# Small parameters and sinks issued from GpSimd's queue, the sinks negated after the second norm, normed activations written for both token halves by one instruction

## The chip, the core and the metric

The kernel runs on one core of a Trainium2 chip. The metric is the device time of one execution in microseconds, as the median of several runs; lower is better. One further execution was recorded by the hardware profiler, and all rows below come from it.

## What is computed

One layer of a hybrid encoder, for 512 prompt tokens and 128 sample tokens (8 requests of 16), D = 1024, everything in float32:

```python
x = x + 0.5 * swiglu(rms_norm(x, norm_ffn1), w_ffn1_up, w_ffn1_down)      # FF = 2816
h = rms_norm(x, norm_mix);  P = h @ w_in                                  # 10752 columns
A = sliding-window attention(q, k, v, sinks)                              # 16 heads of 64
B = HGRN2 recurrence;  C = conv(4) -> RG-LRU * gelu gate
x = x + (sig(gA)*A@w_attn_o + sig(gB)*B@w_hgrn_o + sig(gC)*C@w_lru_o) @ w_out
x = x + 0.5 * swiglu(rms_norm(x, norm_ffn2), w_ffn2_up, w_ffn2_down)

def sink_softmax(s, sinks):
    m = max(max(s), sinks)
    p = exp(s - m)
    return p / (sum(p) + exp(sinks - m))
```

The sinks are one learned number per head; the kernel needs them, and their negatives, in the attention stage only.

## The kernel before

All activations lie transposed: features on the 128 partitions, the T = 640 tokens (512 and 128) on the free axis, in 8 tiles of features. A product is made as two halves of 320 tokens (`HT`), each in its own PSUM bank (`pp`, four banks). Precision comes from splitting: a float32 matrix is rounded to a high part (`wh`, a cast) and a rest (`wl`, a subtraction), and three matmuls (high by high, high by rest, rest by high) replace one. So each weight block of 128 columns (`proj`) is loaded (`wr`, three buffers), cast (L743, on ScalarE or VectorE), subtracted (L744, on VectorE), and multiplied by 24 matmuls (4 feature tiles) or 48 matmuls (8).

Each SwiGLU is made in four chunks of the hidden columns (`CHUNKS`: 4, 6, 6 and 6 blocks). The first chunk uses plain `proj`; the others use a scheme of seven products for eight (`pair`) that reads sums and differences of quarter blocks of the normed activations. These are prepared by `combos`, after the first block of the first chunk: it writes the normed activations x * gain * rstd into buffers `vx`, in two instructions per feature tile, one for each half of the tokens, and then makes sums, casts and rests of them.

Small parameters (norm gains, convolution, gates, q and k norms: 13 transfers) are loaded into a staging tile by `load_params`, called through `more_params` by `ffn` before block 4, and after block 8 is begun its `place` transposes them on TensorE (L441) into the tile `PRM`. They wait for RS, the first norm's result. The sinks go into the tile `SK` by 10 transfers in `attention`, each of which broadcasts numbers that lie 8 bytes apart to 16 or 64 partitions; they wait for `PRM`. One VectorE instruction (L374, called from `attention`) then writes the negated sinks.

The order of all instructions is not written by hand. Each call records an operation with its engine, its assumed duration and its data dependencies; `Sched.run` then plays a list schedule: at each step it takes the operation that could start first, by its assumed costs, and among those within 0.04 us the one with the best priority, and emits it. So the order on each engine is fixed when the program is built, by the planner's times and not by real ones, and each engine runs its list in order: if the first instruction of a list waits, all behind it wait. In this order the negation of the sinks stands on VectorE among the down-projections of the first chunk, long before the attention stage, because the planner takes the sinks to have landed by then. All transfers but one parameter load are issued by the SP queue (`dma`, L413), which is in order too.

Of the kernel before, what the change touches and what calls it, by code (L numbers as in the profile page):

```python
# [16 lines left out]
P = 128  # L17
# [139 lines left out]
class Sched:  # L157
# [4 lines left out]
    LAT_PE = 0.24  # L162
    LAT_TO_PE = 0.55
    LOAD = 1.35
    TO_R = 0.09
    RESIZE = 0.1

# [96 lines left out]
    def run(self):  # L264
        engines = ("PE", "DVE", "ACT", "POOL", "SP")
        free = dict.fromkeys(engines, 0.0)
        ready = {e: {} for e in engines}
        loaded, dma_free, mode = "none", 0.0, (True, P)
        tables = dict(TABLES, none=())

        def enlist(o):
            for a in o.alts:
                ready[a[0]][id(o)] = o

        for o in self.ops:
            if o.npred == 0:
                enlist(o)
        for _ in range(len(self.ops)):
            best = None
            for e in engines:  # L280
                cands = []
                for o in ready[e].values():
                    at, slots = (0.0, ()) if not o.news else self._place(o)
                    if at is not None:
                        sw = e == "ACT" and o.func is not None and o.func not in tables[loaded]
                        cands.append((max(free[e], o.ready, at) + (self.LOAD if sw else 0.0), o, slots))
                if not cands:
                    continue
                t0 = min(c[0] for c in cands)
                if best is not None and t0 >= best[0]:  # L290
                    continue
                near = [c for c in cands if c[0] <= t0 + 0.04]

                def key(c):
                    sw = e == "ACT" and c[1].func is not None and c[1].func not in tables[loaded]
                    if e == "PE" and c[1].mode[0] != mode:
                        return c[1].prio + 0.3 * 1e5
                    return c[1].prio + (0.35e5 if sw else 0.0)

                for c in sorted(near, key=key):  # L300
                    o = c[1]
                    if len(o.alts) > 1:
                        mine = c[0] + next(a[1] for a in o.alts if a[0] == e)
                        if min(max(free[a[0]], c[0]) + a[1] for a in o.alts if a[0] != e) < mine - 0.2:
                            continue
                    best = (c[0], e, o, c[2])
                    break
            if best is None:
                raise RuntimeError(self.stuck())
            start, e, o, slots = best  # L310
            dur, fn = next((a[1], a[2]) for a in o.alts if a[0] == e)
            if e == "ACT" and o.func is not None and o.func not in tables[loaded]:
                loaded = next(n for n, fs in TABLES.items() if o.func in fs)
            if e == "PE":
                start += self.TO_R if o.mode[0][0] and not mode[0] else 0.0
                start += self.RESIZE if o.mode[0][1] != mode[1] else 0.0
                mode = o.mode[1]
            end = start + dur
            free[e] = end
            if o.dma:  # L320
                dma_free = max(dma_free, start + 1.3) + o.dma / 250e3
                end = dma_free + 0.8
            for b, s in zip([b for b in o.news if b.slot is None], slots):
                b.slot, b.ap, s.owner = s, s.place(), b
                b.tag.next += 1
            for a in o.alts:
                ready[a[0]].pop(id(o), None)
            fn()
            o.done = True
            for b in o.bufs:  # L330
                b.left -= 1
                b.end = max(b.end, end)
                if b.left == 0 and b.slot is not None:
                    b.slot.owner, b.slot.free = None, b.end
            lat = self.LAT_PE if e == "PE" else self.LAT
            for s in o.succ:
                to_pe = s.alts[0][0] == "PE"
                s.ready = max(s.ready, end + (lat if not to_pe else 0.0 if e == "PE" else self.LAT_TO_PE))
                s.npred -= 1
                if s.npred == 0:  # L340
                    enlist(s)
# [3 lines left out]
def trunk_kernel(ctx: ExitStack, tc: tile.TileContext, A: dict, O: list):  # L345
# [12 lines left out]
    def act(n, f, aps=0, src=None):  # L358
        return ("ACT", 0.1 + 0.833e-3 * n + 0.093 * aps - (0.049 if src is not None and src.in_psum else 0.0), f)
# [25 lines left out]
    def fn(out, a, func, scale=1.0, bias=0.0, accum=None):  # L385
        aps = isinstance(scale, View) + isinstance(bias, View) + (accum is not None)
        kw = {}

        def f():
            if accum is not None:  # L390
                kw["accum_out"] = accum()
            nc.scalar.activation(out(), a(), func, bias=ap_of(bias), scale=ap_of(scale), **kw)  # L392

        return S.op([act(out.n, f, aps, a)], [a, scale, bias], [out] + ([accum] if accum is not None else []),
                    func=None if func in ANY_TABLE else func)

    def cp(out, a, only=None):
# [10 lines left out]
        alts = [pol(out.n, lambda: nc.gpsimd.memset(out(), val)), dve(out.n, lambda: nc.vector.memset(out(), val))]  # L408
        return S.op(pick(alts, only), (), [out])

    def dma(out, a, lag=None, after=(), act=False):
        v = out if isinstance(out, View) else a
        alts = [("SP", 0.47, lambda: nc.sync.dma_start(ap_of(out), ap_of(a)))]  # L413
        if act:
            alts = [("ACT", 0.47, lambda: nc.scalar.dma_start(ap_of(out), ap_of(a)))]
        return S.op(alts, [a, *after], [out], dma=v.n * 4 * v.proto.shape[0], lag=lag)

    def mm(calls):
# [82 lines left out]

    def combos_tags(sfx, ry, rx, at):

        S.tag("vx" + sfx, RW.slots(rx - 1, 0, T, 6) + of_ar(at, T, 4))
        S.tag("vB" + sfx, RX.slots(rx, 0, 2560, 2) + RY.slots(ry, 0, 2560, 1))
        arena(at, [("vS" + sfx, 512, 3), ("vr" + sfx, 1024, 1)])
        in_region(RW, rx, [("vh" + sfx, 512, 4), ("vl" + sfx, 512, 4)])
# [96 lines left out]
    def load_params(names, r0, r1, lag=None, act=False):  # L604
        b = S.buf("pst")
        later = () if act else (RS.v,)
        for name, r, c in (("norm_ffn1", 0, 8), ("norm_mix", 8, 8), ("norm_ffn2", 16, 8), ("conv_b", 24, 8),
                           ("conv_w", 32, 32), ("lru_b_a", 64, 8), ("lru_b_x", 72, 8), ("lru_lambda", 80, 8),
                           ("hgrn_lb_logits", 88, 8), ("hgrn_o_norm", 96, 1)):
            if name in names:  # L610
                src = A[name][0].rearrange("j (k p) -> (j k) p", p=P) if name == "conv_w" else A[name].rearrange("o (k p) -> (o k) p", p=P)
                dma(b[r - r0:r - r0 + c, 0:P].at(r), src, lag=lag, after=later, act=act)
        for r, name in ((97, "q_norm"), (98, "k_norm")):
            if name in names:
                for h in range(2):
                    dma(b[r - r0:r - r0 + 1, h * 64:h * 64 + 64].at((r, h)), A[name], lag=lag, after=later)

        def place():
            ps = S.buf("ml")
            n = r1 - r0  # L620
            tr([(ps[:, :n], b[:n, :P], ident[:n, :n])])
            cp(PRM[:, r0:r1].at(r0), ps[:, :n], only=("DVE",))

        if not act:
            return place
        place()
# [143 lines left out]
    def combos(norm, R, sfx):  # L770

        vs = [S.buf("vx" + sfx).v for _ in range(8)]
        for k in range(KD):
            h, q = k // 4, (k % 4) // 2
            for n in range(2):
                o = vs[(h * 2 + q) * 2 + n].r("p (a b) -> p a b", a=2)[:, k % 2, :].at(k % 2)
                stt(o, hv(xk(k))[:, n, :], prm(norm + k), hv(RS.v)[:, n, :], ALU.mult, ALU.mult)

        def x(h, n, q):
            return vs[(h * 2 + q) * 2 + n]

        def put(dst, q, v):
            hi, lo = dst(0, q), dst(1, q)
# [9 lines left out]
        vb = [in_b(S.buf("vB" + sfx)) for _ in range(3)]  # L795
        ops = {"x11": in_r(0), "x21": in_r(1), "x22": in_r(2), "t1": in_r(3), "t2": vb[0], "t3": vb[1], "t4": vb[2]}
        for q in range(2):
            a, b = S.buf("vx" + sfx), S.buf("vx" + sfx)
            tt(a.v, x(1, 1, q), x(0, 1, q), ALU.subtract)
            put(ops["t3"], q, a.v)  # L800
            tt(b.v, x(0, 1, q), x(0, 0, q), ALU.subtract)
# [165 lines left out]
    def attention():  # L967
        ck, cv = A["cache_attn_k"][0], A["cache_attn_v"][0]
        sk = A["attn_sinks"][0].rearrange("(m two) -> two m", two=2)
        for h in range(2):  # L970
            dma(SK[h * 64:h * 64 + 64, 0:8].at(h), sk[h:h + 1, :].to_broadcast([64, 8]), after=(PRM.v,))
            for b in range(4):
                p0 = b * 32 + h * 16
                dma(SK[p0:p0 + 16, 8:16].at((b, h)), sk[h:h + 1, :].to_broadcast([16, 8]), after=(PRM.v,))
        ts(SK[:, 16:32], SK[:, 0:16], -1.0, ALU.mult, only=("DVE",))
        ms = S.buf("ms")
        mi = S.buf("qt")
        i1, i2 = mi[:, 0:256].cast(I32), mi[:, 256:512].cast(I32)
# [504 lines left out]
```

## Time and profile before

| | us |
|---|---|
| median of 3 runs | 1932.46 (1931.64 to 1934.26) |
| the profiled execution, its own time | 1930.95 |
| its span, first to last instruction | 1929.1 |
| TensorE busy in it | 1895.8 (98%) |
| VectorE busy | 1388.1 (72%) |
| ScalarE busy | 740.3 (38%) |
| GpSimd busy | 36.4 (2%) |
| mean granted TensorE clock | 0.994 |

The 1.85 us between the span and the execution's own time lie around the first and last instruction. TensorE is the engine to look at: the span is its work plus the stretches in which it waits, and the stretches in which its clock is lowered. The other engines matter where they make it wait.

### The profile page before, as it was taken

To read this page: it belongs to the slowest core of one execution; us is meant where nothing else is said; L and a number is where in the kernel's file an instruction comes from. 1 tells how busy PE (TensorE), PEld (TensorE's weight loads), DVE (VectorE), ACT (ScalarE), POOL (GpSimd) and SP (SyncE) were. 2 spreads that over 40 slices of the span, in tenths; PEclk is the share of its full clock that TensorE was granted. 3 is DMA by queue.
4 is the path that set the end of the run, shared out by engine and by line. 5 is a ranking of instruction groups with operands and counts; after the bars stand their busy time and mean duration, and the time that the engine had idled before them with its cause. 6 is when DMAs were issued, how large, how long until landed. Compare 5 with 4: busy or idle time off the path is not lost.

```text
span 1929.1 us, 35224 instructions
## 1 busy us (share of the span) xinstructions
PE 1895.8 (98%) x14654; PEld 1851.0 (96%) x14654; DVE 1388.1 (72%) x2610; ACT 740.3 (38%) x1299; POOL 36.4 (2%) x63
## 2 busy tenths in 40 slices
PE   8899999999999999999999999999999999999999
PEld 8789999999999999999999999999999999999998
DVE  7788585877687773778547787886566989586784
ACT  6334141433477750776102343434112324142340
POOL 0000000000000000021000000000000000000000
PEclk9999999999999999999999999999999999999999
DMA  5133222225322112223221332232422133222322
GB/s 143 43 96 92 80 82 73 87 73 152 102 56 61 50 55 77 61 67 91 77 77 57 88 93 82 77 87 72 132 77 76 54 101 88 88 64 80 99 64 80
DMA packets 305130, 156.89 MB, mean 81 GB/s; under 512 B 22949, under 2 KB 302598, under 8 KB 304970
## 3 DMA queue, kind: packets, MB, share of 16 engines
q1 hardware_dynamic: 304954, 154.63, 27.8%
q8 instruction: 115, 1.88, 0.4%
q14 instruction: 45, 0.37, 0.1%
q10 hardware_dynamic: 16, 0.00, 0.0%
HBM read 143.32 MB, written 10.63 MB: 80 GB/s over the span
## 4 chain that ended last, share of the span: by engine, by line
PE 94%; DVE 2%; DMA 1%; ACT 1%; issue 0%; SPq 0%; DVEq 0%; ACTq 0%
PE pp L432 85%; PE me L432 4%; PE ml L432 3%; PE ml L441 1%; PE me L441 1%; DMA SK<-in_attn_sinks_dram 1%; DVE AR L368 1%; ACT AR L392 1%; DVE AR L1222 0%; ACT L392 0%; DVE AR L382 0%; DMA RX<-in_x_prompt_dram 0%; SPq L413 0%; DVE wl L744 0%; DVE RB L368 0%
## 5 line engine op out<-in xcount | busy, mean ns | idle before, releaser
L432 PE MATMUL pp<-RA,wh 128*128 128x320 f32 x4192 | 813.1, 313 | 0.3 <-DVE AR L368 0.3
L432 PEld LDWEIGHTS pp<-RA,wh 128*128 128x128 f32 x4192 | 658.1, 188 | 12.5 <-issue 9.5
L432 PE MATMUL pp<-RA,wl 128*128 128x320 f32 x2096 | 490.1, 309 | 4.5 <-DVE wl L744 4.5
L432 PE MATMUL pp<-RB,wh 128*128 128x320 f32 x2016 | 389.6, 310 | 13.5 <-DVE AR L382 12.7
L432 PEld LDWEIGHTS pp<-RA,wl 128*128 128x128 f32 x2096 | 354.0, 188 | 5.5 <-DVE wl L744 5.5
L432 PEld LDWEIGHTS pp<-RB,wh 128*128 128x128 f32 x2016 | 320.4, 188 | 14.8 <-DVE AR L382 13.3
L743 DVE CAST wh<-wr 128x1024 fp32r<-128x1024 f32 (+2 forms) x135 | 85.5, 633 | 237.5 <-PE pp L432 237.0
L432 PE MATMUL pp<-RB,wl 128*128 128x320 f32 x1008 | 241.9, 309 | 1.3 <-DVE wl L744 1.3
L744 DVE TENSOR_TENSOR wl<-wr,wh 128x1024 fp32r<-128x1024 f32 (+2 forms) x196 | 217.0, 1107 | 1.4 <-ACT wh L743 1.0
L831 ACT CAST RW<-AR 128x512 fp32r<-128x512 f32 x180 | 110.5, 621 | 259.6 <-PE pp L432 131.2
L432 PEld LDWEIGHTS pp<-RB,wl 128*128 128x128 f32 x1008 | 172.0, 188 | 1.5 <-DVE wl L744 1.5
L368 DVE TENSOR_TENSOR AR<-AR 128x640 f32<-128x640 f32 (+12 forms) x271 | 139.5, 519 | 24.8 <-ACT AR L392 15.7
L368 DVE TENSOR_TENSOR AR<-pp,AR 128x320 f32<-128x320 f32 x268 | 127.9, 486 | 34.4 <-PE pp L432 31.6
L392 ACT ACTIVATE AR<-AR 128x640 f32<-128x640 f32 (+2 forms) x184 | 110.6, 605 | 108.3 <-DVE AR L368 99.3
L432 PE MATMUL pp<-RX,RW 128*128 128x320 f32 x864 | 138.6, 309 | 0.0
L432 PEld LDWEIGHTS pp<-RX,RW 128*128 128x128 f32 x864 | 129.6, 188 | 0.0
L828 DVE TENSOR_TENSOR RW<-AR,RW 128x512 fp32r<-128x512 f32 x180 | 122.4, 686 | 2.0 <-ACT RW L831 0.7
L392 ACT ACT_TABLE_LOAD x72 | 92.4, 1283 | 2.5 <-PEq L1471 1.4
L743 ACT CAST wh<-wr 128x1024 fp32r<-128x1024 f32 (+2 forms) x61 | 59.7, 979 | 50.3 <-PE pp L432 49.9
L398 ACT COPY AR<-me 128x512 f32<-128x512 f32 (+3 forms) x74 | 26.8, 378 | 123.4 <-PE me L441 115.0
L382 DVE SCALAR_TENSOR_TENSOR AR<-pp,AR 128x320 f32<-128x320 f32 x128 | 61.4, 484 | 15.5 <-PE pp L432 15.5
L432 PE MATMUL pp<-RY,RW 128*128 128x320 f32 x432 | 69.2, 309 | 0.0
(184 smaller groups left out, 1953.1 us busy)
## 6 DMA issues: line engine op xcount, KB each, us to landing
wr<-in_w_in_dram SPq DMA_DIRECT2D x84, 512.0 KB
wr<-in_w_ffn_up_dram SPq DMA_DIRECT2D x52, 512.0 KB
AR<-in_w_ffn_up_dram SPq DMA_DIRECT2D x36, 512.0 KB
wr<-in_w_ffn_down_dram SPq DMA_DIRECT2D x48, 384.0 KB
wr<-in_w_ffn_down_dram SPq DMA_DIRECT2D x16, 256.0 KB
wr<-in_w_attn_o_dram SPq DMA_DIRECT2D x8, 512.0 KB
AR<-in_state_hgrn_dram SPq DMA_DIRECT2D x8, 512.0 KB
wr<-in_w_lru_o_dram SPq DMA_DIRECT2D x8, 512.0 KB
```

What stands on the lines that cost most here:

```text
L368: alts = [dve(out.n, lambda: nc.vector.tensor_tensor(out(), a(), b(), op=op))]
L382: return S.op([dve(out.n, lambda: nc.vector.scalar_tensor_tensor(out(), a(), ap_of(s), b(), op0=op0, op1=op1), isinstance(s, View))], [a, ...
L392: nc.scalar.activation(out(), a(), func, bias=ap_of(bias), scale=ap_of(scale), **kw)
L398: alts = [act(out.n, lambda: nc.scalar.copy(out(), a()), 0, a), dve(out.n * (1.0 if a.in_psum else 0.5), lambda: nc.vector.tensor_copy(out ...
L432: nc.tensor.matmul(o(), l(), m(), start=s, stop=e)
L441: nc.tensor.transpose(o(), i(), d())
L743: S.op([act(nk * P, lambda: nc.scalar.copy(h(), r())), dve(nk * P * 0.5, lambda: nc.vector.tensor_copy(h(), r()))], [r], [h], lag=2)
L744: S.op([dve(nk * P, lambda: nc.vector.tensor_tensor(l(), r(), h().bitcast(F32), op=ALU.subtract))], [r, h], [l], lag=1.5)
L828: S.op([dve(out.n, lambda: nc.vector.tensor_tensor(out(), a(), b(), op=op))], [a, b], [out], lag=lag)
L831: S.op([act(out.n, lambda: nc.scalar.copy(out(), a()))], [a], [out], lag=lag)
```

## The change

Four things change in the code.

1. The 13 parameter transfers and the 10 sink transfers are issued by GpSimd's queue (`small=True`, assumed cost 1.0 us each on POOL) instead of SP's. The first parameter load, norm_ffn1, stays on ScalarE's queue.
2. The negation of the sinks is recorded as reading RS as well as SK, after the second norm has written RS anew; so it can be planned only behind the second norm.
3. `combos` writes the normed activations with one instruction per feature tile for all 640 tokens (8 in place of 16, in each SwiGLU). The buffers `vx` become four of 2T in place of ten of T, and the two work buffers get a tag of their own, `vy`.
4. Two assumed costs of the planner change: no transfer lands before 5.5 us (`FIRST`), and a ScalarE instruction with an accumulated sum is taken as 0.1 us longer. No instruction is added by this; the emitted order can differ.

```diff
+    FIRST = 5.5
...
-        loaded, dma_free, mode = "none", 0.0, (True, P)
+        loaded, dma_free, mode = "none", self.FIRST, (True, P)
...
-        return S.op([act(out.n, f, aps, a)], [a, scale, bias], [out] + ([accum] if accum is not None else []),
+        alt = act(out.n, f, aps, a)
+        if accum is not None:
+            alt = (alt[0], alt[1] + 0.1, f)
+        return S.op([alt], [a, scale, bias], [out] + ([accum] if accum is not None else []),
                     func=None if func in ANY_TABLE else func)
...
-    def dma(out, a, lag=None, after=(), act=False):
+    def dma(out, a, lag=None, after=(), act=False, small=False):
...
+        if small:
+            alts = [("POOL", 1.0, lambda: nc.gpsimd.dma_start(ap_of(out), ap_of(a)))]
...
-        S.tag("vx" + sfx, RW.slots(rx - 1, 0, T, 6) + of_ar(at, T, 4))
+        S.tag("vx" + sfx, RW.slots(rx - 1, 0, 2 * T, 3) + of_ar(at, 2 * T, 1))
+        S.tag("vy" + sfx, of_ar(at + 2 * T, T, 2))
...
-                dma(b[r - r0:r - r0 + c, 0:P].at(r), src, lag=lag, after=later, act=act)
+                dma(b[r - r0:r - r0 + c, 0:P].at(r), src, lag=lag, after=later, act=act, small=not act)
...
-                    dma(b[r - r0:r - r0 + 1, h * 64:h * 64 + 64].at((r, h)), A[name], lag=lag, after=later)
+                    dma(b[r - r0:r - r0 + 1, h * 64:h * 64 + 64].at((r, h)), A[name], lag=lag, after=later, small=True)
...
-        vs = [S.buf("vx" + sfx).v for _ in range(8)]
+        vs = [S.buf("vx" + sfx) for _ in range(4)]
         for k in range(KD):
-            h, q = k // 4, (k % 4) // 2
-            for n in range(2):
-                o = vs[(h * 2 + q) * 2 + n].r("p (a b) -> p a b", a=2)[:, k % 2, :].at(k % 2)
-                stt(o, hv(xk(k))[:, n, :], prm(norm + k), hv(RS.v)[:, n, :], ALU.mult, ALU.mult)
+            o = vs[k // 2].v.r("p (n a b) -> p n a b", n=2, a=2)[:, :, k % 2, :]
+            stt(o, hv(xk(k)), prm(norm + k), hv(RS.v), ALU.mult, ALU.mult)
...
-            dma(SK[h * 64:h * 64 + 64, 0:8].at(h), sk[h:h + 1, :].to_broadcast([64, 8]), after=(PRM.v,))
+            dma(SK[h * 64:h * 64 + 64, 0:8].at(h), sk[h:h + 1, :].to_broadcast([64, 8]), after=(PRM.v,), small=True)
...
-        ts(SK[:, 16:32], SK[:, 0:16], -1.0, ALU.mult, only=("DVE",))
+        S.op([dve(16, lambda: nc.vector.tensor_scalar(SK[:, 16:32](), SK[:, 0:16](), -1.0, None, op0=ALU.mult))], [SK.v, RS.v], [SK.v])
```

## Rows read from the trace of the kernel before

**Rows 1.** The page: busy time of each engine; shares of the chain that ended last.
```profile
PE 1895.8 (98%) x14654; PEld 1851.0 (96%) x14654; DVE 1388.1 (72%) x2610; ACT 740.3 (38%) x1299; POOL 36.4 (2%) x63
...
PE 94%; DVE 2%; DMA 1%; ACT 1%; issue 0%; SPq 0%; DVEq 0%; ACTq 0%
```

**Rows 2.** Waits of PE, whole span: total us, times, longest.
```profile
PE pp L432 <- DVE AR L382: 12.7, 2, 12.3
PE pp L432 <- DVE wl L744: 5.7, 5, 2.7
PE me L441 <- DMA RX<-in_x_prompt_dram: 4.1, 2, 2.0
```

**Rows 3.** Windows by stage: length, busy us of each engine, clock, DMA share, GB/s.
```profile
core 0: us, PE busy (x) PEld busy (x) DVE busy (x) ACT busy (x) POOL busy (x), PEclk, DMA share, GB/s
...
31.00:75.00 44.00, 44.00 (x302) 43.99 (x301) 43.44 (x70) 18.76 (x27) 0.00 (x0) 1.00 0.22 62
...
88.15:107.60 19.45, 6.80 (x33) 6.45 (x33) 7.34 (x29) 0.21 (x1) 0.00 (x0) 0.65 0.25 68
107.60:117.60 10.00, 10.00 (x74) 9.81 (x72) 9.27 (x19) 4.02 (x6) 0.00 (x0) 1.00 0.59 173
125.00:475.00 350.00, 350.00 (x2388) 350.00 (x2388) 260.54 (x437) 124.99 (x198) 4.20 (x6) 1.00 0.31 90
...
790.00:903.00 113.00, 107.13 (x704) 105.28 (x703) 91.74 (x172) 92.05 (x119) 21.35 (x26) 0.97 0.22 64
```

**Rows 4.** Timeline of 74 to 101 us: start, us, engine, line, operation [idle before].
```profile
74.77 0.24 PE L441 MATMUL ml<-ident,AR 91*128 91x91 f32 x1
...
76.89 0.56 PE L432 MATMUL pp<-RB,wl 128*128 128x320 f32 x2 [1.25 <-DVE wl L744]
...
99.20 0.18 DVE L374 TENSOR_SCALAR SK<-SK 128x16 f32<-128x16 f32 x1 [15.42 <-DMA SK<-in_attn_sinks_dram]
...
100.44 0.64 PE L432 MATMUL pp<-RB,wh 128*128 128x320 f32 x1 [12.29 <-DVE AR L382]
```

**Rows 5.** The chain of waits, 70 to 105 us: start, us, what.
```profile
77.28 8.69 DMA SK<-in_attn_sinks_dram
...
89.86 9.11 DMA SK<-in_attn_sinks_dram
```

**Rows 6.** Windows of 2 us around the longest wait, columns as in the third group.
```profile
84.00:86.00 2.00, 2.00 (x16) 2.00 (x15) 0.00 (x0) 0.00 (x0) 0.00 (x0) 1.00 0.05 0
...
92.00:94.00 2.00, 0.00 (x0) 0.00 (x0) 0.00 (x0) 0.00 (x0) 0.00 (x0) 0.50 0.20 44
...
104.00:106.00 2.00, 2.00 (x13) 2.00 (x13) 1.56 (x9) 0.21 (x1) 0.00 (x0) 0.79 0.22 64
```

**Rows 7.** Timeline of the SP queue: parameter issues (first, last), then sink issues.
```profile
31.20 0.48 SPq L413 DMA_DIRECT2D AR<-in_norm_mix_dram  x1
...
35.92 0.55 SPq L413 DMA_DIRECT2D AR<-in_k_norm_dram  x2
...
77.28 4.85 SPq L413 DMA_DIRECT2D SK<-in_attn_sinks_dram  x7
82.23 0.39 SPq L413 DMA_DIRECT2D wr<-in_w_ffn_down_dram  x1
```

**Rows 8.** Timeline of DVE: normed activations by halves, and the nearest whole-width instruction.
```profile
1504.37 2.40 DVE L382 SCALAR_TENSOR_TENSOR RW<-AR,PRM,RS 128x320 f32<-128x320 f32 x5
...
16.64 1.68 DVE L382 SCALAR_TENSOR_TENSOR RA<-AR,PRM,RA 128x640 fp32r<-128x640 f32 x2 [0.83 <-ACT RA L392]
```

**Rows 9.** Timeline of PE in the second SwiGLU's first chunk.
```profile
1546.06 0.56 PE L432 MATMUL pp<-RA,wl 128*128 128x320 f32 x2 [1.22 <-DVE wl L744]
```

**Rows 10.** Instructions that read the tile SK: count, ns min/median/max, first and last start.
```profile
L376 DVE TENSOR_SCALAR AR<-AR,SK x40: 206/224/423, 525.9 to 695.4; 128x2 f32<-128x2 f32 x40
```

**Rows 11.** Line L392 on ACT: the extra instruction of an accumulated sum, startup.
```profile
L392 ACT ACTIVATION_READ_ACCUMULATOR AR<-RX x20: 185/187/216, 4.9 to 25.3; 128x1 f32 x20
```

**Rows 12.** Lines of DVE by form, 77 to 100 us: the casts of weight blocks.
```profile
L743 DVE CAST wh<-wr 128x512 fp32r<-128x512 f32 x3 | 1.3, 424 | 0.6 <-PE pp L432 0.5
```

More of the change, by code (lines that the diff above doesn't have):

```diff
@@ L770, in combos @@
     def combos(norm, R, sfx):
-        vs = [S.buf("vx" + sfx).v for _ in range(8)]
+        vs = [S.buf("vx" + sfx) for _ in range(4)]
         for k in range(KD):
-            h, q = k // 4, (k % 4) // 2
-            for n in range(2):
-                o = vs[(h * 2 + q) * 2 + n].r("p (a b) -> p a b", a=2)[:, k % 2, :].at(k % 2)
-                stt(o, hv(xk(k))[:, n, :], prm(norm + k), hv(RS.v)[:, n, :], ALU.mult, ALU.mult)
+            o = vs[k // 2].v.r("p (n a b) -> p n a b", n=2, a=2)[:, :, k % 2, :]
+            stt(o, hv(xk(k)), prm(norm + k), hv(RS.v), ALU.mult, ALU.mult)
         def x(h, n, q):
-            return vs[(h * 2 + q) * 2 + n]
+            return vs[h * 2 + q][:, n * T:(n + 1) * T]
         def put(dst, q, v):
@@ L797, in combos @@
         for q in range(2):
-            a, b = S.buf("vx" + sfx), S.buf("vx" + sfx)
+            a, b = S.buf("vy" + sfx), S.buf("vy" + sfx)
             tt(a.v, x(1, 1, q), x(0, 1, q), ALU.subtract)
@@ L970, in attention @@
         for h in range(2):
-            dma(SK[h * 64:h * 64 + 64, 0:8].at(h), sk[h:h + 1, :].to_broadcast([64, 8]), after=(PRM.v,))
+            dma(SK[h * 64:h * 64 + 64, 0:8].at(h), sk[h:h + 1, :].to_broadcast([64, 8]), after=(PRM.v,), small=True)
             for b in range(4):
                 p0 = b * 32 + h * 16
-                dma(SK[p0:p0 + 16, 8:16].at((b, h)), sk[h:h + 1, :].to_broadcast([16, 8]), after=(PRM.v,))
-        ts(SK[:, 16:32], SK[:, 0:16], -1.0, ALU.mult, only=("DVE",))
+                dma(SK[p0:p0 + 16, 8:16].at((b, h)), sk[h:h + 1, :].to_broadcast([16, 8]), after=(PRM.v,), small=True)
+        S.op([dve(16, lambda: nc.vector.tensor_scalar(SK[:, 16:32](), SK[:, 0:16](), -1.0, None, op0=ALU.mult))], [SK.v, RS.v], [SK.v])
         ms = S.buf("ms")
```

## The prediction

> **What bounds the kernel.** I read the page first. TensorE (PE) is busy 1895.8 of 1929.1 us and carries 94% of the chain that ended last [rows 1]. So the span is PE's work plus 33.3 us of idling, and a change can only pay where PE waits or runs at a low clock. The second view is the list of PE's waits: the largest entry is 12.7 us in two waits for VectorE (DVE) at L382, one of 12.3; next come 5.7 in five waits for weight rests [rows 2]. The third view is the windows by stage: from 31 to 75 us and from 125 to 475 us PE has no gap; 88.15 to 107.6 holds only 6.80 busy us in 19.45; 790 to 903 lacks 5.9 [rows 3].
>
> The long wait is then followed back. In the timeline PE starts again at 100.44 after 12.29 us idle; it waited for a DVE eviction, but DVE itself had stood 15.42 us before a tiny instruction at 99.20, the negation of the sinks, which waited for their transfers [rows 4]. The chain of waits shows these from 77.28 to 98.97 (89.86 + 9.11) [rows 5]. So ten transfers, 21.7 us from the first issue to the last landing, 2.17 each, block DVE's whole list, although their first reader starts at 525.9 [rows 10]. The reader should see that the engine named in PE's wait is not the culprit: the culprit is an instruction ahead of it in DVE's list whose data nobody needs yet.
>
> The clock adds to it. At 84 to 86 the granted clock is 1.00 (2.4 GHz), after some microseconds without matmuls 0.50 (1.2 GHz), and in 104 to 106 still 0.79 [rows 6]; PE, back at work from 100.44, is slow there.
>
> **The change part by part.**
>
> *Negation behind the second norm.* Its wait leaves the stretch. At full clock PE does 2388 matmuls in 350 us, 0.1466 each [rows 3]. In 88.15 to 107.6 it did 33, worth 33 x 0.1466 = 4.84 us, so 19.45 - 4.84 = 14.6 us are lost: the two idles of 12.7 and some 2 us of half clock [rows 2, 3, 6]. Is something else late in the gap? DVE was standing, not working, so its list simply moves forward. Right after, in 107.6 to 117.6, DVE does such work at 9.27 of 10 us with PE without a gap at clock 1.00 [rows 3], so DVE can feed PE, though with little room. The weight block that SP issued at 82.23 stood behind seven sink issues of 4.85 us [rows 7]; without them it goes out sooner, so weights are not late either. Term: -14.6, bounds -13.3 (with DVE's room so thin, one wait for a weight rest like the 1.25 us at 76.89 [rows 4] recurs) to -14.6. At its new place the instruction costs DVE at most its own 0.18 us [rows 4], somewhere near 480 to 526, where DVE is not known to hold PE: 0, bounds 0 to +0.2. Behind it stands the rest of DVE's attention work, but the sinks have been landed for hundreds of microseconds by then, unless GpSimd needs (525.9 - 77.3) / 10 = 45 us for each.
>
> *Sinks on GpSimd's queue.* SP loses 10 issues (two groups; the first seven 4.85 us [rows 7]). GpSimd's queue (POOL) gets 10 and has nothing else to do there: it is busy 36.4 us in all and idle in every stage from 31 to 118 us [rows 1, 3]. The same small packets still cross the same DMA engines, whose share in 84 to 86 was 0.05 [rows 6]. Cost 0, bounds 0 to +6 (the contention rival).
>
> *Parameters on GpSimd's queue.* SP loses 13 issues between 31.20 and 36.47 [rows 7]; PE had no gap until 75, so that gives 0. The receiver is the transpose at 74.77 in PE's list [rows 4]. From 31.20 that leaves 43.6 us, 3.35 for each of 13 if they go strictly one after another. No row shows a POOL-issued transfer. Nearest rows: 0.41 per issue on SP (5.27 / 13), below; 2.17 per sink transfer through landing, above [rows 5, 7]. At 2.17 the last lands at 31.2 + 28.2 = 59.4, 15 us early. Cost 0, bounds 0 to what the second rival says.
>
> The row that bears on interference: DVE is busy 43.44 of 44 us in 31 to 75, exactly where POOL would issue [rows 3]; the trace shows no POOL work there, so no interference can be read. The Trainium skill, page "SBUF — State Buffer", section "SBUF: two separate sides", speaks against this edit: descriptors of a transfer issued from GpSimd are written through a port that some VectorE copies hold, and it gives about 620 ns alone against about 3100 ns beside a float32 copy. By that figure the 13 would take 40.3 us and be done at 71.5 (an estimate from that page), 3.3 us before the transpose, and the sum would stand unchanged; no run here shows it yet.
>
> *Normed activations in one instruction.* Sixteen instructions of 320 columns become eight of 640, twice in the kernel. A run of five takes 2.40 us, 0.48 each; two of 640 columns with a per-partition scalar take 1.68, 0.84 each [rows 8]. So 16 x 0.48 - 8 x 0.84 = 1.0 us of DVE per SwiGLU. In the first one DVE is full up to the 1.25 us wait for a weight rest at 76.89 [rows 3, 4], so DVE's saving reaches PE: -1.0, bounds 0 to -1.25. In the second, the same wait is 1.22 us [rows 9], but more has happened between; I take -0.3, bounds 0 to -1.2.
>
> *Planner's costs.* The real extra instruction of an accumulated sum takes 0.187 us [rows 11], so the planner comes nearer to the truth; a late first landing shifts all its transfers alike and should leave their order. PE outside the long wait idles 33.3 - 12.7 = 20.6 us; a new order can shrink or stretch any of it. 0, bounds -3 to +3 (half the 5.9 of 790 to 903, each way).
>
> **Sum.** From the profiled execution's own 1930.95: -14.6 - 1.0 - 0.3 = 1915.05, 15.9 less. The median of the runs shown, 1932.46, lies 1.5 above that execution, so a median of 1932.46 - 15.9 = 1916.5. A measurement of this kernel tells about 0.2% (3.9 us) from no change.
>
> **Rivals.**
>
> *Contention: part of the gain is lost.* POOL's sink transfers hold up DVE's casts, or delay weight loads, just where PE used to stand. For it: DVE's room there is only 0.73 us in 10 [rows 3]. Against it: DMA share 0.05 [rows 6], and casts take only 0.42 us each [rows 12]. Price: in 21.7 us PE does 21.7 / (24 x 0.1466) = 6 weight blocks; if each cast waits for one transfer of 2.17 that is 13 us on DVE, less its room of 1.6, so up to 11.4; half of it, 5.7, gives 1922.
>
> *Parameters late: slower.* The transpose at 74.77 stands in PE's in-order list, all projections behind it. If a POOL transfer takes d, PE waits 13 d - 43.6 us; up to 3.35 it costs nothing, at 4.57 it eats the 15.9, and at 5 it costs 21.4, which gives 1938. For it: DVE is full then, and the last sink transfers took 9.11 us from issue to landing [rows 3, 5]. Against: that was latency and many small packets, while these are whole rows, and 13 in line at 2.17 are 15 us early. The Trainium skill's figure above lies just below the limit.
>
> *No change.* The negation goes, but another wait of that length appears: the DVE list held back by something else, or the order redrawn badly. Nothing in the rows names it; about 1931.
>
> *More gain.* The redrawn order also closes part of the 5.9 us in 790 to 903 [rows 3] and of the startup waits of 4.1 [rows 2]: 1910.
>
> **How the numbers follow.** Forecast (1912.5 to 1919.5, from -3 to +3 of the order) 0.65; contention (1919.5 to 1928) 0.15; more gain 0.08; no change 0.05; slower 0.07. The range 1911 to 1926 takes the forecast, most of contention and the near part of more gain: a little over 0.8. Faster by over 0.2% (below 1928.6): 0.65 + 0.15 + 0.08 = 0.88. Within: 0.05 and a little of the slower case, 0.06. Slower: 0.06.
>
> **What the new profile would show.** Right: the negation of the sinks stands after 478 us with no idle before it; PE's wait for L382 near 88 us is gone and the clock stays 1.00 from 31 to 118 us; 16 instructions of 640 columns write `vx` where 32 of 320 did; the parameter transpose has no wait before it. Wrong: PE waiting at a transpose L441 near 75 us (parameters late); DVE casts longer than 0.42 us or idle before them between 77 and 110 (contention); waits for weights there; or a longer list of PE's waits in 475 to 903 (order). If POOL's transfers take over 4.57 us each, the sign is wrong.

## The result

The changed kernel takes 1922.38 us, the median of 6 runs (1919.91 to 1924.02), against 1932.14 for the kernel before beside it (6 runs, 1930.95 to 1934.26). The ratio is 0.9946, with a 95% interval of 0.9936 to 0.9956: 9.8 us less, of the 15.9 forecast. The forecast was 1916.5, in a range of 1911 to 1926. The profiled execution took 1923.28 us, span 1921.5, which is 7.67 below the profiled execution of before (7.64 by the spans).

Page of the changed kernel, the row that answers to [rows 1] and the DMA queue that only kernels with transfers on POOL have (packets, MB, share of 16 engines):

```profile
PE 1898.9 (99%) x14654; PEld 1853.0 (96%) x14654; DVE 1389.1 (72%) x2599; ACT 735.8 (38%) x1295; POOL 44.3 (2%) x86
...
q0 software_dynamic: 736, 0.06, 0.4%
```

Its waits of PE over the whole span, which answer to [rows 2]:

```profile
PE pp L438 <- DVE wl L751: 6.4, 5, 2.4
PE me L447 <- DMA RX<-in_x_prompt_dram: 4.6, 2, 2.6
```

The long wait for an eviction is gone. The five waits for weight rests have grown from 5.7 to 6.4 us. PE's busy time has also grown, by 3.1 us with the same 14654 matmuls: part of the gain went into slower matmuls.

Windows by stage, with the columns of [rows 3]:

```profile
31.00:75.00 44.00, 44.00 (x304) 44.00 (x304) 41.14 (x60) 19.52 (x28) 0.53 (x1) 1.00 0.25 72
75.00:79.00 4.00, 2.41 (x18) 2.14 (x16) 4.00 (x7) 1.37 (x2) 0.00 (x0) 1.00 0.00 0
80.00:82.00 2.00, 2.00 (x10) 2.00 (x10) 2.00 (x6) 0.79 (x2) 0.00 (x0) 0.59 0.49 139
82.00:84.00 2.00, 2.00 (x10) 2.00 (x10) 1.60 (x6) 0.91 (x2) 0.00 (x0) 0.55 0.15 44
...
94.00:108.00 14.00, 14.00 (x100) 13.77 (x100) 12.47 (x26) 4.58 (x7) 0.00 (x0) 1.00 0.63 185
...
1538.00:1540.00 2.00, 2.00 (x10) 2.00 (x9) 2.00 (x6) 0.00 (x0) 0.00 (x0) 0.50 0.38 111
```

From 94 to 108 PE works without a gap at the full clock, where [rows 3] show 6.80 busy us in 19.45. New is what follows the waits for weight rests: from 80 to 84 the granted clock is 0.59 and 0.55 of 2.4 GHz, ten matmuls in 2 us where there would be sixteen, and 0.50 from 1538 on in the second SwiGLU.

Timeline of PE, then of DVE, around the first of these waits, and the negation's new place:

```profile
76.52 0.24 PE L447 MATMUL ml<-ident,AR 91*128 91x91 f32 x1
...
78.97 0.56 PE L438 MATMUL pp<-RB,wl 128*128 128x320 f32 x2 [1.59 <-DVE wl L751]
```

```profile
69.74 2.29 DVE L369 TENSOR_TENSOR RA<-RW,RA 128x640 fp32r<-128x640 f32 x3 [1.37 <-PE pp L438]
...
72.69 0.82 DVE L369 TENSOR_TENSOR RW<-RW 128x640 f32<-128x640 f32 x1
...
77.50 0.82 DVE L369 TENSOR_TENSOR RW<-RW 128x640 f32<-128x640 f32 x1
78.23 0.68 DVE L751 TENSOR_TENSOR wl<-wr,wh 128x512 fp32r<-128x512 f32 x1
...
468.31 0.17 DVE L980 TENSOR_SCALAR SK<-SK 128x16 f32<-128x16 f32 x1
```

The parameter transpose L447 waits for nothing; the negation stands at 468.31 with no idle before it. But DVE runs without a pause from 69.74, when PE releases rows of RA, to the weight rest at 78.23, and two subtractions within `RW` stand in that run, 0.82 us each. They come back below.

Timeline of the POOL queue (start, us):

```profile
2.85 0.66 POOL L421 DMA_DIRECT2D AR<-in_norm_mix_dram  x1 [1.54 <-PE ml L447]
...
11.32 0.96 POOL L421 DMA_DIRECT2D AR<-in_k_norm_dram  x2
12.27 1.81 POOL L421 DMA_DIRECT2D SK<-in_attn_sinks_dram  x3
...
32.15 0.53 POOL L421 DMA_DIRECT2D SK<-in_attn_sinks_dram  x1 [6.24 <-issue]
```

This is the surprise of the profile: the parameters are issued from 2.85 us on and the sinks from 12.27 to 32.15, not near 31 and 77 as on SP. `after=(RS.v,)` and `after=(PRM.v,)` order the planner's list, but the rows show no wait behind them: the first issue waits only for a transpose of the start, and the sinks go out long before PRM is written near 81. On SP the issues came late because they stood behind others in the queue. POOL's queue holds nothing else there, so they run at once.

**Where the time went.** The n-th of the 14654 matmuls can be set beside the n-th of before. The table gives by how much each stretch is longer (+) or shorter (-) than in the trace of before, in us, in one profiled execution of each kernel; the ranks 100, 500, 550, 650, 3400, 4750, 12000 and 12250 start at 23, 83, 106, 120, 524, 691, 1535 and 1573 us there. "sum - start" leaves out the first stretch, which varies for a reason that stays open (below). All thirteen are single executions; the medians stand beside them.

| kernel | to 100 | to 500 | to 550 | to 650 | to 3400 | to 4750 | to 12000 | to 12250 | sum - start | median us |
|---|---|---|---|---|---|---|---|---|---|---|
| changed | +1.75 | +1.88 | -14.92 | +0.01 | +0.01 | +1.48 | -0.04 | +2.18 | -9.40 | 1922.38 |
| e0 | +2.49 | +1.87 | -14.92 | +0.01 | 0.00 | +1.12 | -0.02 | +2.18 | -9.77 | 1923.52 |
| e1 | +1.45 | 0.00 | -14.92 | +9.36 | 0.00 | +0.01 | +0.82 | 0.00 | -4.72 | 1926.62 |
| e2 | +0.99 | +0.34 | -14.93 | +9.84 | -0.01 | +1.13 | -0.11 | +0.65 | -3.10 | 1930.28 |
| e3 | +1.05 | 0.00 | -14.93 | +0.01 | 0.00 | +1.20 | +0.92 | 0.00 | -12.82 | 1918.75 |
| e4 | +2.66 | +1.89 | -14.93 | +0.01 | +0.01 | +0.04 | +1.34 | +2.17 | -9.48 | 1920.51 |
| e5 | +1.27 | +0.34 | -14.92 | +6.40 | +0.01 | +1.14 | +0.19 | +2.18 | -4.67 | 1927.69 |
| e6 | +1.42 | -0.30 | -14.92 | +0.01 | 0.00 | +1.49 | +1.53 | 0.00 | -12.22 | 1918.49 |
| e7 | +2.43 | +0.01 | -14.92 | +0.01 | +0.01 | 0.00 | -0.08 | 0.00 | -15.00 | 1917.06 |
| e8 | -0.37 | -0.30 | -14.92 | +0.01 | -0.02 | -0.07 | -0.45 | 0.00 | -15.75 | 1916.18 |
| e9 | +1.91 | 0.00 | -14.92 | +0.01 | +11.73 | -0.02 | +1.73 | 0.00 | -1.50 | 1929.74 |
| e10 | +1.83 | 0.00 | -14.92 | 0.00 | -0.01 | -0.05 | -0.25 | +0.01 | -15.25 | 1916.94 |
| e11 | +0.72 | -0.30 | -14.92 | 0.00 | 0.00 | -0.04 | -0.44 | 0.00 | -15.72 | 1917.40 |

In the changed kernel's row the long wait is worth 14.92 us, and three things eat into it: 1.88 at the first wait for a weight rest, 1.48 in attention, 2.18 at the wait in the second SwiGLU. The experiments look for the cause of each.

### The profile page after: what moved, and what is told of

The parts are those of the page before. It is cut to its first block, busy times and chain, and to the rows that moved or that the text cites. A ratio compares the mean times of both kernels' runs of the same rounds, so it can differ in the third digit from the quotient of the medians.

```text
span 1921.5 us, 35215 instructions
## 1 busy us (share of the span) xinstructions
PE 1898.9 (99%) x14654; PEld 1853.0 (96%) x14654; DVE 1389.1 (72%) x2599; ACT 735.8 (38%) x1295; POOL 44.3 (2%) x86
## 3 DMA queue, kind: packets, MB, share of 16 engines
q8 instruction: 115, 1.88, 0.4%
## 4 chain that ended last, share of the span: by engine, by line
PE 93%; DVE 4%; ACT 2%; issue 1%; DMA 1%; SPq 0%; ACTq 0%; DVEq 0%
PE pp L438 84%; PE me L438 4%; PE ml L438 3%; PE ml L447 1%; PE me L447 1%; DVE AR L383 1%; ACT AR L393 1%; DVE AR L369 1%; DVE RB L369 0%; DVE AR L1227 0%; ACT L393 0%; DMA RX<-in_x_prompt_dram 0%; DVE wl L751 0%; SPq L417 0%; DVE RA L369 0%
## 5 line engine op out<-in xcount | busy, mean ns | idle before, releaser
L750 DVE CAST wh<-wr 128x1024 fp32r<-128x1024 f32 (+2 forms) x142 | 89.4, 630 | 237.2 <-PE pp L438 236.5
L750 ACT CAST wh<-wr 128x1024 fp32r<-128x1024 f32 (+1 forms) x54 | 53.7, 994 | 36.9 <-PE pp L438 36.5
```

The source lines that it names most:

```text
L750: S.op([act(nk * P, lambda: nc.scalar.copy(h(), r())), dve(nk * P * 0.5, lambda: nc.vector.tensor_copy(h(), r()))], [r], [h], lag=2)
```

## The experiments

**The negation alone.** e1 is the kernel before with only the negation's line changed:

```diff
-        ts(SK[:, 16:32], SK[:, 0:16], -1.0, ALU.mult, only=("DVE",))
+        S.op([dve(16, lambda: nc.vector.tensor_scalar(...))], [SK.v, RS.v], [SK.v])
```

> The kernel before with the negation of the sinks alone moved behind the second norm; everything else, all transfers on SP's queue too, as before. Theory A (the negation's move carries the whole gain, the other parts cost a little): the 12.3 us wait near 88 us and the half clock behind it go, 14.9 us less, so about 1917, 5 us below the changed kernel. Rival B (GpSimd's queue is needed as well: the ten sink issues still stand in SP's queue among the weight loads from 77 to 91 us): TensorE then waits some microseconds for a weight block between 85 and 105 us, and the time lies at 1920 to 1926.

Measured: 1926.62, ratio 0.9964 [0.9951, 0.9976]. The old wait is gone, and a new one of 6.93 us stands at 100.05: rival B's wait, at a time 0.6 us above its range. DVE of e1, its SP queue, the chain of waits (start, us, what) and a window of the DMA engines:

```profile
99.17 0.43 DVE L743 CAST wh<-wr 128x512 fp32r<-128x512 f32 x1 [10.01 <-DMA wr<-in_w_ffn_down_dram]
```

```profile
78.72 4.92 SPq L413 DMA_DIRECT2D SK<-in_attn_sinks_dram  x7
83.75 0.38 SPq L413 DMA_DIRECT2D wr<-in_w_ffn_down_dram  x1
87.42 5.06 SPq L413 DMA_DIRECT2D SK<-in_attn_sinks_dram  x3
```

```profile
83.75 15.33 DMA wr<-in_w_ffn_down_dram
```

```profile
84.00:92.00 8.00, 8.00 (x57) 8.00 (x56) 4.49 (x21) 0.00 (x0) 0.00 (x0) 1.00 0.05 0
```

The negation no longer waits for the sinks, but a cast now waits 10.01 us for a weight block. That block was issued at 83.75, behind the first seven sinks, and landed only 15.33 us later; from 84 to 92 the DMA engines were busy 0.05 of the time and moved 0 GB/s. The packet records show none of its packets on the move before 93. So it was not issued late: it stood behind the sinks' packets, on engines that were nearly idle. In the trace of before the same block went out at 82.23 [rows 7] while DVE stood until 99.20, so this second delay was hidden under the first. The transfers must move too.

**All on SP.** e2 is the changed kernel with the small transfers on SP (`if small:` replaced by `if False:`).

> The changed kernel with the 23 small transfers back on SP's queue. In the changed kernel's trace they were issued at 2.9 to 32 us, while the activations were loaded, and TensorE's list ran 1.75 us late from 45 us on. Theory A (small transfers among the first loads cost the startup): TensorE's 250th matmul starts at 45.0 as before instead of 46.7, 1.75 us less, about 1920.5. Rival B (the planner's new costs made the startup later): it stays at 46.7 and the time at 1922 or, if SP's queue is blocked by the sinks, above.

Measured: 1930.28, ratio 0.9985 [0.9977, 0.9994]: the loss of e1 is back (+9.84 in the table), as rival B allowed. On the start the run decides nothing (+0.99).

**The normed activations by halves.** e3 is the changed kernel with that part undone:

```diff
-        vs = [S.buf("vx" + sfx) for _ in range(4)]
+        vs = [S.buf("vx" + sfx).v for _ in range(8)]
...
+            for n in range(2):
+                stt(o, hv(xk(k))[:, n, :], prm(norm + k), hv(RS.v)[:, n, :], ALU.mult, ALU.mult)
```

> The changed kernel with the normed activations written by halves again, 16 instructions with the buffers of before. Theory A (the 1.0 us saved on VectorE is lost where it waits for TensorE to release the normed activations' old rows, before the wait for a weight rest): the waits for weight rests at 77 and 1535 us stay at 1.2 to 1.7 us, time within 2 us of the changed kernel, 1920 to 1924. Rival B (the forecast: VectorE's saving reaches TensorE): 1.3 to 2 us slower than the changed kernel, waits longer by 1 us each.

Measured: 1918.75, ratio 0.9922 [0.9909, 0.9936]. Both waits for weight rests are back at 1.26 and 1.22 us, the clock is 1.00 behind both, and the +1.88 and +2.18 of the table are 0. Neither theory had that: in these traces the one instruction for both halves did not save 1.3 us, it cost 4.1.

Most of the 4.1 is the clock, and not the waits themselves. e2 has the same instruction and the same first wait. PE of e2, and its window behind the wait:

```profile
78.21 0.56 PE L438 MATMUL pp<-RB,wl 128*128 128x320 f32 x2 [1.60 <-DVE wl L751]
```

```profile
80.00:82.00 2.00, 2.00 (x16) 2.00 (x15) 2.00 (x6) 1.54 (x3) 0.00 (x0) 1.00 0.26 63
```

Here the clock stays 1.00, also behind the second wait of 1.72, and the table has +0.34 and +0.65. So the longer waits cost 1.0 us together, and the fallen clock of the changed kernel 1.5 at each place.

**Why: a dependency that is none.** With both halves in one buffer, the subtraction that overwrites the second half is planned to wait for every reader of the buffer, the first half's too, which wait for PE to release RA. e6 is the changed kernel with one word more, by which a reader names its half:

```diff
-            return vs[h * 2 + q][:, n * T:(n + 1) * T]
+            return vs[h * 2 + q][:, n * T:(n + 1) * T].at(n)
```

> The changed kernel with the normed activations still made for both halves of the tokens in one instruction, but with their readers naming the half that they read, so that the subtraction of the two halves no longer has to wait until the first half's last reader is done. Theory A (this false dependency put the subtractions into the burst of VectorE ahead of wl and made wl late): the waits of PE for wl fall from 1.59 and 1.7 to 1.2 or less, the clock near 80 us and 1538 us stays at full speed, 1917.5 to 1919.5, the level of the kernel that makes them by halves (1918.75) or up to 1.3 less. Theory B (the whole-width instruction itself, or a cast that the planner gave to VectorE, makes wl late): the waits stay at 1.5 to 1.7 and the time at 1921 to 1923.

Measured: 1918.49, ratio 0.993 [0.9916, 0.9943], beside the changed kernel itself (e0: 1923.52, ratio 0.9952 [0.9939, 0.9964]): Theory A. Timeline of e6, DVE and then PE, and its window behind the wait:

```profile
64.64 0.82 DVE L369 TENSOR_TENSOR RW<-RW 128x640 f32<-128x640 f32 x1
...
69.42 2.30 DVE L369 TENSOR_TENSOR RA<-RW,RA 128x640 fp32r<-128x640 f32 x3 [1.33 <-PE pp L438]
...
77.42 0.68 DVE L751 TENSOR_TENSOR wl<-wr,wh 128x512 fp32r<-128x512 f32 x1
```

```profile
78.16 0.56 PE L438 MATMUL pp<-RB,wl 128*128 128x320 f32 x2 [1.10 <-DVE wl L751]
```

```profile
80.00:82.00 2.00, 2.00 (x16) 2.00 (x15) 1.78 (x5) 1.35 (x2) 0.00 (x0) 1.00 0.20 55
```

The subtractions stand ahead of the release of RA, the last at 64.64, where the trace of before has one at 64.26. The wait is 1.10 and the clock stays 1.00. The order alone did it: the instruction for both halves is still there. A cast of 0.42 us, which the changed kernel has on DVE at 74.16 within that run, went to ScalarE with the same edit, so its part and that of the two subtractions are not told apart.

> The changed kernel itself on the chip of the three kernels below, so that they can be compared with it: 1922.4 us before, expected 1921 to 1924. Its lateness at the 100th matmul against the first trace of the kernel before was +1.75 us; if that belongs to the transfers on POOL it comes again here and in the keyed kernel (+1.5 to +2), if it is the scatter of one execution it may be anything from 0 to 2.7.

e0's first 100 matmuls were 2.49 us late and e6's 1.42: scatter of that size leaves the question of the start open.

**The planner's costs.** e4 is the changed kernel with `FIRST` at 0 and without the 0.1 us for an accumulated sum.

> The changed kernel with the planner's two assumed costs as before (no first landing at 5.5 us, no 0.1 us more for accumulated sums). In the changed kernel the attention stage lost 1.5 us against the order of before (lead of 11.3 us at 490 us, 9.8 at 691). Theory A (the accumulated sums' new cost redrew that stage): the lead stays 11.3 us through the stage, about 1921. Rival B (the startup order was improved by the costs, or nothing depends on them): 1922 to 1924, lead 9.8 again.

Measured: 1920.51, ratio 0.9932 [0.9919, 0.9944]. The time is not told apart from the changed kernel's, but its loss in attention is, as Theory A had it: +0.04 instead of +1.48. In the table all six kernels with the 0.1 us (e0, e2, e3, e5, e6 and the changed one) lose 1.12 to 1.49 there, and all seven without it lose nothing. Hardly any wait is behind this (from 505 to 682 us e3 lists 0.2 us of PE waits) and the clock there is 1.00: the matmuls stand in another order. Which step of that order costs the time was not looked for. e7 takes e3's halves and the old cost of the sum together, and keeps `FIRST`:

> The changed kernel with the normed activations made by halves, as in the kernel before, and with the planner's old cost of an activation that sums; the negation behind the second norm, the transfers on POOL and the planner's first free time of the DMA stay. Theory A (the planner's cost cost 1.2 to 1.5 us in attention, and adds to the halves' gain): no loss between the 3400th and the 4750th matmul, 1916.5 to 1918, the fastest so far. Theory B (each plan is drawn anew and the two don't add): 1918 to 1921.

Measured: 1917.06 (1916.43 to 1918.38), ratio 0.9922 [0.991, 0.9935], attention 0.00: Theory A. e8 does the same with e6's one instruction:

> The changed kernel with whole-width normed activations whose readers name their half (1918.49 in the last call) and the planner's old cost of an activation that sums. Theory A (the two gains stand in different stages and add, as with the kernel by halves, which went from 1918.75 to 1917.06): 1916 to 1917.5, level with the kernel by halves or up to 1 us under it. Theory B (the one instruction for both halves saves nothing even without its false dependency, and the planner's cost changes where the plan was lucky): 1917.5 to 1920.

Measured: 1916.18 (1914.83 to 1917.22), ratio 0.9913 [0.99, 0.9927], the lowest median of all, though not told apart from e7's. Since e3 and e7 differ by the 0.1 us alone, and e6 and e8 too, this assumed cost is shown to be the cause.

**Queue or time.** e5 leaves the transfers on POOL but gives each group a real wait, a POOL copy of one column in front of it:

```diff
+        S.op([pol(1, lambda: nc.gpsimd.tensor_copy(GT.ap, RS[:, TP:TP + 1]()))], [RS.v], [GT.v])
...
+        S.op([pol(1, lambda: nc.gpsimd.tensor_copy(GS.ap, PRM[:, 8:9]()))], [PRM.v], [GS.v])
```

> The changed kernel with the small transfers still on POOL, but the parameters behind a POOL copy that reads the first norm's result, and the sinks behind a POOL copy that reads PRM, so that they are issued near 30 us and near 80 us, as on SP, and not from 2.9 us on. Theory A (what hurt in the kernel with the negation alone was SP's queue, in which the sinks stand ahead of the feed-forward weights): the weights are still issued early, no wait of PE for more than 2 us near 100 us, 1921 to 1924 as in the changed kernel. Theory B (the sinks' packets of 4 bytes slow the weights' packets on the DMA engines, whatever queue issues them): a wait of 4 to 7 us near 100 us is back, 1926 to 1929. Beside this: if the early transfers made the start 1 to 1.75 us late, the 100th matmul comes that much earlier here than in the changed kernel.

Measured: 1927.69, ratio 0.9977 [0.9968, 0.9986]: Theory B by the time. Here the sinks run where the forecast had put them, from 81 us on, and PE loses 6.40 us behind them. Window 81 to 95 of e5, and then of the changed kernel, whose sinks are long over by then:

```profile
81.00:95.00 14.00, 14.00 (x97) 14.00 (x96) 11.83 (x46) 1.65 (x3) 5.26 (x10) 1.00 0.70 57
```

```profile
81.00:95.00 14.00, 14.00 (x89) 14.00 (x88) 11.53 (x44) 1.91 (x4) 0.00 (x0) 0.90 0.26 76
```

The DMA engines are busy 0.70 of the time for 57 GB/s, against 0.26 for 76. The queues of e5 from 60 to 110 us, and then what DVE waits for behind them:

```profile
q1 hardware_dynamic: 8410, 4.32, 29.2%
q0 software_dynamic: 320, 0.01, 14.7%
```

```profile
101.79 0.69 DVE L835 TENSOR_TENSOR AR<-AR,wr 128x512 f32<-128x512 f32 x1 [5.67 <-DMA wr<-in_w_ffn_up_dram]
```

320 packets with 0.01 MB take 14.7% of 16 engines for 50 us, 118 us of engine time or 0.37 us each on average. The weight blocks of w_ffn_up in these 50 us land late, at a median of 6.9 us against 4.0 in the changed kernel. That is not what e1 shows: on SP the engines were nearly idle and the weights stood behind the sinks, here the sinks' packets keep the engines busy. So Theory B's "whatever queue issues them" does not hold for the way in which the weights are held up. Two kernels then leave POOL out altogether. Both are e1 with the sinks elsewhere in SP's queue. e9 asks for the second norm, so they stand behind it:

```diff
-            dma(SK[...].at(h), sk[h:h + 1, :].to_broadcast([64, 8]), after=(PRM.v,))
+            dma(SK[...].at(h), sk[h:h + 1, :].to_broadcast([64, 8]), after=(RS.v,))
```

> The kernel before with the negation behind the second norm and the ten sinks still on SP, but asked to wait for the second norm's result, so that they stand in SP's queue among the projections' weights near 470 to 490 us and no longer near 77 us. Theory A (the time at which the sinks' small packets run decides, not the queue): no wait over 2 us near 100 us, 1917.5 to 1921 unless the weights of the projections are now late in their turn; in that case a wait of 3 to 10 us near 480 to 520 us. Theory B (the sinks must leave SP's queue): 1925 or more with the wait near 100 us as it was.

Measured: 1929.74, ratio 0.9983 [0.9974, 0.9992]. Nothing is lost near 100 us, but 11.73 us are lost near 490. Theory A allowed for a wait there and put it down to late weights; it comes by the mechanism of the kernel before, the negation in DVE's list. DVE and PE of e9:

```profile
485.94 0.17 DVE L975 TENSOR_SCALAR SK<-SK 128x16 f32<-128x16 f32 x1 [13.87 <-DMA SK<-in_attn_sinks_dram]
```

```profile
490.10 0.64 PE L432 MATMUL me<-NL,bd 128*128 128x320 f32 x1 [8.40 <-DVE NL L368]
```

e10 moves the same lines of code up to the parameters, with `after=(RS.v,)` of the first norm, so that they stand right behind these in SP's queue:

> The kernel before with the negation behind the second norm and the ten sinks still on SP, but right behind the parameters, near 37 us, where SP next stands still for 16 us with a weight block that waits for its buffer. Theory A (the time decides, not the queue): no wait of PE over 2 us near 100 us nor before it, 1917 to 1920, as good as the changed kernel's POOL queue with the old halves (1918.75). Theory B (on SP the sinks hold up weights wherever they stand): a wait of 3 to 10 us somewhere between 40 and 70 us or near 100 us, 1922 or more.

Measured: 1916.94 (1916.66 to 1917.54), ratio 0.9915 [0.9902, 0.9929]: Theory A. The SP queue of e10:

```profile
38.25 3.27 SPq L413 DMA_DIRECT2D SK<-in_attn_sinks_dram  x4
41.61 0.39 SPq L413 DMA_DIRECT2D wr<-in_w_ffn_up_dram  x1
42.05 8.09 SPq L413 DMA_DIRECT2D SK<-in_attn_sinks_dram  x6
50.25 14.84 SPq L413 DMA_DIRECT2D wr<-in_w_ffn_down_dram  x3
```

The sinks hold SP for 11.4 us here too. The next weight issues are not hurt: in the trace of before three of them take 15.95 us from 47.31, since each waits for its buffer, and here 14.84 from 50.25. With the negation and this move alone, nothing on POOL, and activations and costs as they were, the median is 5.4 us under that of the changed kernel (ratio 0.9915 against 0.9946). So the time at which the sinks run decides: issued near 80 us they cost 9.36 us from SP (e1) and 6.40 from POOL (e5), and issued before 51 us nothing that the table shows behind the start (e10 and the changed kernel).

e11 adds e6's one instruction with named halves to e10:

> The kernel before with the negation behind the second norm, the ten sinks on SP right behind the parameters (1916.94 with the normed activations by halves), and the normed activations for both halves in one instruction whose readers name their half; nothing on POOL and the planner's costs as before. Theory A (without its false dependency the whole-width instruction saves what the forecast gave it, 1.3 us): 1915 to 1916.5, level with the fastest kernel so far (1916.18), which has the transfers on POOL. Theory B (the instruction's saving is spare time of VectorE): 1916.5 to 1918.

Measured: 1917.4 (1915.97 to 1919.13), ratio 0.9923 [0.9909, 0.9936]: Theory B by the median, and not told apart from e10. In the table it is 0.30 us shorter than e10 at the first weight rest and 0.47 in all without the start.

## Why the forecast was right, point by point

The time lies inside the range, 5.9 us above the forecast, in the band that it gave to the contention rival (1919.5 to 1928). That rival is not what happened. The main mechanism was right and carries the result; one term had the wrong sign, one was put at nothing, and the zero for the sinks on POOL held by luck, because they ran far earlier than the forecast took them to. Of its signs one failed: the clock did not stay 1.00 up to 118 us. Its sums come out, but for one edge: 1912.5 lies 4 us under 1916.5, not the 3 that it names.

- **The long wait, -14.6: right (-14.92), on a condition.** The forecast booked the gain under the negation and let the weight block behind the sinks go out sooner once these had left SP ("so weights are not late either"). e1 prices that condition at 9.36 us: with the sinks on SP the block landed 15.33 us after its issue. And leaving SP would not have been enough at 77 us, as e5 shows. The gain needs both moves, the negation behind the norm and the sinks away from that time.
- **Sinks on POOL, 0: right in size, by luck.** The forecast read `after=` as a wait, let POOL issue them from 77 us and found no work there to disturb. It also took the share of 0.05 that "the same small packets" had on SP for their share on POOL; in e5 the share is 0.70. At that time they cost 6.40 us (e5), near the 5.7 of the contention rival, though through late weights more than held-up casts. They cost nothing because all had been issued by 32.15 us, in an otherwise empty queue. The Trainium skill, page "DMA: Bandwidth & Descriptors", section "Issuing engines are not separate DMA queues", says that transfers share the same DMA engines whichever engine issues them, and that another issuer saves only the time to issue. e5 agrees that another issuer is no way around: on POOL at 81 us 6.40 of the 9.36 us remain.
- **Parameters on POOL, 0: right.** They were issued from 2.85 to 12.3 us and landed within 5.3 to 6.7 us, so nothing was late at the transpose. The forecast's test, 4.57 us for each, took them to go one after another; here they were issued about 0.5 us apart and overlapped, so longer landings cost nothing. In e5, where they ran when the forecast had meant them to, the transpose was not late either: issued from 33.75 on beside a DVE that was busy 8.00 of 8 us, they took 0.49 to 0.67 us each to issue and landed after 1.6 to 3.6. The price that the page "SBUF — State Buffer" of the Trainium skill, section "SBUF: two separate sides", led the forecast to weigh, 3.1 us beside a VectorE copy, is not in these rows; what ran on DVE there was subtractions and products with one copy out of PSUM, so the page's own case was hardly tested.
- **Normed activations, -1.0 and -0.3: wrong in sign.** They cost 1.88 and 2.18 us, of which 0.34 and 0.65 are the longer waits and the rest is the clock, as far as e2 shows. DVE does save: in the first SwiGLU twelve instructions of half width keep it busy 5.9 us and six of whole width 5.1. But the saving fell ahead of 69.74, where DVE then waits 1.37 us for RA (0.46 at 68.00 in the trace of before), and the merged buffer put subtractions behind that release. The forecast counted busy time on an engine that is full on average and didn't look at which buffer each reader then holds. With the dependency mended the term is -0.30 and 0.00 (e6, e8, e11).
- **Planner's costs, 0 with bounds of 3 each way: mis-sized.** The costlier accumulated sum loses 1.1 to 1.5 us in attention; nothing measurable came from `FIRST`: no column of the table tells e7 and e8, which have it, from e10 and e11, which don't, beyond the scatter.
- **Start, 0: open.** The changed kernel's first 100 matmuls are 1.75 us late, and the early POOL transfers among the loads of x look guilty. It isn't shown: against the one trace of before, kernels with the small transfers on SP are late by 0.72 to 1.91, those with early POOL transfers by -0.37 to 2.66, and the gated e5 by 1.27.

Sum by the traces: -14.92 + 1.88 + 1.48 + 2.18 + 1.75 = -7.63, against 7.64 measured between the spans of the two profiled executions. The medians differ by 9.8 because the changed kernel's profiled execution lies 0.9 above its median and that of before 1.2 below.

## What to carry to other kernels

When a stalled instruction is moved, ask what else the same transfers were delaying, for that becomes the next wait; a trace shows only the longest of two overlapping delays. Put many-packet loads into a stretch where the weight queue waits for its buffers anyway: two small edits on SP (e10) did more than a second queue. And before merging two buffers into one, list who reads and who overwrites each half: a tracker that knows only the whole makes the writer of one half wait for readers of the other, and in an in-order engine that delays whatever stands behind.

## What the runs showed of the hardware

The ten sink transfers of 0.5 to 2 KB hold up weights in two ways. On SP their packet records show some 2000 packets of 4 bytes; the DMA engines are busy 0.05 of the time, and a weight block issued behind seven of the transfers lands after 15.33 us (e1). On POOL they are 320 packets that take 118 us of engine time beside the weights (e5). The average of 0.37 us hides two kinds: in the packet records 32 packets of 128 bytes take 3.6 us each, 114 us together, and the other 288 take 0.01 to 0.02 us.

PE's clock: behind a wait of 1.59 to 1.61 us for a weight rest near 78 us the granted clock fell to 0.50, which is 1.2 GHz, in the changed kernel, e0 and e4; in e2 and e5 it stayed 1.00. Behind the wait of 1.71 or 1.72 near 1540 us it fell in the changed kernel, e0, e4 and e5 and stayed 1.00 in e2. Behind the waits of 1.10 to 1.26 at the two places it stayed 1.00 in the kernel before and in the eight kernels that have them. So the longer wait is what lets the clock fall here, but like waits don't always do it; what decides is not shown. Where it fell, it cost about 1.5 us (1.88 less 0.34, 2.18 less 0.65).

The same loss varies elsewhere, at a place at which no edit is aimed. Windows of 785 to 845 us, in e3, the changed kernel and e10:

```profile
785.00:845.00 60.00, 54.86 (x339) 53.70 (x339) 46.72 (x86) 46.08 (x62) 11.90 (x12) 0.91 0.23 66
785.00:845.00 60.00, 54.78 (x348) 53.16 (x347) 49.23 (x93) 46.86 (x62) 9.07 (x12) 0.94 0.20 58
785.00:845.00 60.00, 54.09 (x350) 52.59 (x349) 47.03 (x87) 47.04 (x63) 11.90 (x12) 0.97 0.23 66
```

The mean granted clock there sorts the table's column from rank 4750 to 12000: it is 0.91 in e1, e3, e4, e6 and e9 (+0.82 to +1.73), 0.94 in the kernel before, the changed one, e0, e2, e5 and e7 (-0.11 to +0.19), and 0.97 in e8, e10 and e11 (-0.45 to -0.25). One kernel varies too: the five executions of e4 go from 1917.37 us at a mean clock of 0.999 to 1924.11 at 0.995. So one or two microseconds in a single execution's total may be this alone.
